# Interleaving a sliding-window attention with its projections from the third head group on instead of the second

## The chip, the core and the metric

The kernel runs on one core of one Trainium2 chip. The metric is the device time of one execution in microseconds (us), as the median of several runs. TensorE (PE, with PEld for its weight loads) multiplies, VectorE (DVE), ScalarE (ACT) and GpSimd (POOL) do the rest, and SyncE (SP) issues the DMAs.

## What is computed

Four decoder layers on 256 tokens of width 1024. Each layer is a half SwiGLU, a token mixer, a second half SwiGLU and a gated input. The mixers are, by layer, HGRN2, mLSTM, sliding-window attention and HGRN2 again. The change lies in layer 2 only, in the attention:

```python
def swa_mixer(x, w_qkv, q_gain, k_gain, sinks, w_o):
    q, k, v = jnp.split(x @ w_qkv, [nq, nq + nk], axis=-1)   # 16 query heads, 4 key heads, 64 wide
    q = rmsnorm(q.reshape(B, T, SW_HEADS, SW_HD), q_gain)
    k = rmsnorm(k.reshape(B, T, SW_KV_HEADS, SW_HD), k_gain)
    ...
    s = jnp.einsum('bnqkgd,bnskd->bnkgqs', qb, kk).astype(jnp.float32) * (SW_HD ** -0.5)
    s = s - slopes[:, :, None, None] * dist
    s = jnp.where(valid[None, :, None, None], s, -jnp.inf)
    probs = jax.nn.softmax(jnp.concatenate([s, sink], axis=-1), axis=-1)[..., :-1]
    o = jnp.einsum('bnkgqs,bnskd->bnqkgd', probs.astype(vv.dtype), vv).reshape(B, T, nq)
    return o @ w_o
```

## The kernel before

**Weights.** All weights stream from memory through four 1 MB buffers (`wraw`), each holding two units. ACT rounds a unit to its high part (`wh`, line 253) and DVE subtracts to get the low part (`wl`, line 254); six units of each fit. The program stays three units ahead of the products. Every projection is then three products: high by high, high by low, low by high.

**The attention stage, function `swa`.** The projections run in this order on PE: keys and values (`gemm_rows(x, 512)`), then the queries of four groups of four heads (`gemm_rows(x, 256)`, 48 products each, lines 275 to 277), then the small input projection (`ple_proj`, 48 products, lines 266 to 268), then the output projection (`out_proj`, 192 products, lines 266 to 268). Groups are counted from 0 here: g = 0 is the first. The output projection needs group g's result at its step k0 = 2g, and forces whatever is missing there (`settle`).

After the products of group g, its results are copied (line 1198), squared (1041), summed by DVE (1044), raised to -1/2 on POOL (line 395, in `rsqrt_mean`), and scaled (1048, 1201, 1204). The attention itself is one generator, `attend`. For each group it transposes the queries (`queries`, PE line 1099, evacuated by ACT line 1101), and for each of two token tiles t takes the softmax: four score products, one per head (PE line 1119), each evacuated by DVE (line 1121), then maximum (1127 to 1131), exponentials on ACT (1134), and division on DVE (1137 to 1141). Up to four softmaxes later, `values` transposes the probabilities (PE 1150, ACT 1152), multiplies by the values (PE 1158) and splits the result for the output projection (ACT 253, DVE 254, destinations `slab`).

**What sets the order.** A queue of generators, `bg`, holds such background work. Every product block calls `tick`, which adds to a credit; `advance` runs the next step of the first generator and takes from the credit what the step yields (a bare `yield` costs 1 / `SW_RATE`, that is 0.4; a block of 48 products of a query group gives 2.0). A yielded number, such as `K_WAIT`, lets that much product work pass before the next step. On top of this the tile framework's scheduler settles the order of the instructions of each engine and puts in the waits. Each engine runs its own list strictly in order.

PSUM for the attention's products are two 512-wide tiles (`mis`). The score products of one softmax share such a tile: four heads of 128 keys in tile t = 0, two of 256 keys per tile for t = 1. The product of the next head in a tile waits until DVE has evacuated the head before it.

Of the kernel before, what the change touches and what calls it, by code (L numbers as in the profile page):

```python
# [41 lines left out]
ML_CAP = 15.0  # L42
SW_H, SW_G, SW_D = 16, 4, 64
AHEAD = 3
K_WAIT, Q_WAIT = 2, 0

N_GAIN = 4

# [72 lines left out]
class Kern:  # L121
# [930 lines left out]
    def swa(self, l):  # L1052
# [43 lines left out]
        def queries(g, qn):  # L1096
            ps = self.misc()
            for i in range(4):
                nc.tensor.transpose(ps[:, i * P:(i + 1) * P], qn[:, i * P:(i + 1) * P], self.ident)
            c = (g % 2) * 512  # L1100
            nc.scalar.activation(qT[g // 2][:, c:c + 512], ps, AF.Copy, scale=self.qg)
            yield
# [64 lines left out]
        def attend():  # L1167

            todo = deque()
            for g in range(SW_H // SW_G):  # L1170
                while g not in qns:
                    yield 0.25
                if Q_WAIT:
                    yield Q_WAIT
                yield from queries(g, qns[g][0])
                for t in range(NT):
                    todo.append((g, t, softmax(g, t)))
                    yield
                    if len(todo) > AHEAD:
                        yield from finish(*todo.popleft())  # L1180
            while todo:
                yield from finish(*todo.popleft())

        def finish(g, t, s):
            yield from values(g, t, s)
            if t == NT - 1:
                done.add(g)
            yield
# [4 lines left out]
        for g in range(SW_H // SW_G):  # L1193
            banks = self.gemm_rows(x, 256)
            self.settle(norm)
            qn = self.s512("qn")
            for t in range(NT):
                nc.scalar.copy(out=qn[:, t * 256:(t + 1) * 256], in_=banks[t][0])
            a = self.head_scales([banks[t][0] for t in range(NT)], rc)
            sa = self.small([P, NT * SW_G], "sa", 3)  # L1200
            nc.vector.reciprocal(out=sa, in_=a)
            s3 = sa.rearrange("p (t h) -> p t h", t=NT)
            sl = self.slopes[:, 4 * g:4 * g + 4].rearrange("p (o h) -> p o h", o=1).broadcast_to([P, NT, SW_G])
            nc.vector.tensor_tensor(out=s3, in0=s3, in1=sl, op=ALU.mult)
            qns[g] = qn, a, sa
            if g == 0:
                self.later(attend())
            outs.append((lambda g=g: g in done, self.tiles(oh[g // 2], ol[g // 2])[2 * (g % 2):][:2]))
        self.ple_proj(l)
# [88 lines left out]
```

## Time and profile before

| | us |
|---|---|
| median of 3 runs | 2115.43 |
| lowest, highest | 2112.28, 2116.8 |
| the profiled execution's own time | 2115.12 |
| its span, first to last instruction | 2113.4 |
| PE busy in the span | 2092.2 (99%) |
| DVE, ACT busy | 1541.4 (73%), 1203.2 (57%) |
| attention stage, from the first query product (1260.87) to the first product after the output projection (1357.37) | 96.5 |
| PE busy in that stage, mean granted clock | 93.94, 0.95 |

Times in the rows are us from the span's start. The profile gives each instruction's start and length; PE products overlap in its pipeline, so that a product is listed with about 0.28 us although the next one starts 0.12 us later. A number in square brackets is the time that the engine stood idle before the row, and what released it. The granted clock is 1.00 at 2.4 GHz and 0.50 at 1.2 GHz.

### The profile page before, as it was taken

To read this page: it belongs to the slowest core of one execution; us is meant where nothing else is said; L and a number is where in the kernel's file an instruction comes from. 1 tells how busy PE (TensorE), PEld (TensorE's weight loads), DVE (VectorE), ACT (ScalarE), POOL (GpSimd) and SP (SyncE) were. 2 spreads that over 40 slices of the span, in tenths; PEclk is the share of its full clock that TensorE was granted. 3 is DMA by queue.
4 is the path that set the end of the run, shared out by engine and by line. 5 is a ranking of instruction groups with operands and counts; after the bars stand their busy time and mean duration, and the time that the engine had idled before them with its cause. 6 is when DMAs were issued, how large, how long until landed. Compare 5 with 4: busy or idle time off the path is not lost.

```text
span 2113.4 us, 30586 instructions
## 1 busy us (share of the span) xinstructions
PE 2092.2 (99%) x12269; PEld 1822.3 (86%) x12269; DVE 1541.4 (73%) x2065; ACT 1203.2 (57%) x1678; POOL 50.7 (2%) x84
## 2 busy tenths in 40 slices
PE   8999999999999999999999999999999999999998
PEld 7888889888888888888888887888888888898887
DVE  8766987776877666776687666777687767967766
ACT  7554655554655556655565546665566545565554
POOL 1000000000000000000000001000000000000000
PEclk9999999999999999999999999999999999999999
DMA  7554345555555544555545552355545554445552
GB/s 285 199 186 179 131 149 181 183 196 184 180 197 182 198 142 164 186 192 190 189 179 183 193 181 91 118 193 182 197 170 193 196 183 156 140 160 182 197 182 78
DMA packets 54000, 372.27 MB, mean 176 GB/s; under 512 B 6368, under 2 KB 7136, under 8 KB 9568
## 3 DMA queue, kind: packets, MB, share of 16 engines
q1 hardware_dynamic: 53712, 370.24, 49.1%
q8 instruction: 96, 1.57, 0.3%
q14 instruction: 48, 0.39, 0.1%
q10 hardware_dynamic: 144, 0.07, 0.0%
HBM read 369.23 MB, written 1.05 MB: 175 GB/s over the span
## 4 chain that ended last, share of the span: by engine, by line
PE 89%; DVE 5%; ACT 2%; issue 2%; POOL 1%; DMA 0%; SPq 0%; DVEq 0%; POOLq 0%; ACTq 0%
PE acc L285 50%; PE acc L286 25%; PE acc L267 2%; PE acc L268 2%; PE acc L266 2%; PE acc L275 2%; PE acc L276 2%; PE acc L277 2%; DVE wl L254 1%; PE mis L735 1%; DVE slab L742 1%; PE mis L1119 1%; DVE slab L748 1%; ACT wh L253 0%; PE mis L431 0%
## 5 line engine op out<-in xcount | busy, mean ns | idle before, releaser
L285 PE MATMUL acc<-x,wh 128*128 128x512 f32 x3384 | 1185.2, 395 | 5.9 <-ACT wh L253 5.8
L254 DVE TENSOR_TENSOR wl<-wraw,wh 128x1024 fp32r<-128x1024 f32 (+1 forms) x693 | 845.2, 1222 | 460.5 <-ACT wh L253 460.2
L253 ACT CAST wh<-wraw 128x1024 fp32r<-128x1024 f32 (+1 forms) x693 | 725.8, 1049 | 757.2 <-PE acc L285 412.7
L286 PE MATMUL acc<-x,wl 128*128 128x256 f32 x3384 | 946.1, 280 | 0.6 <-DVE wl L254 0.5
L285 PEld LDWEIGHTS acc<-x,wh 128*128 128x128 f32 x3384 | 635.4, 188 | 153.2 <-ACT wh L253 5.7
L286 PEld LDWEIGHTS acc<-x,wl 128*128 128x128 f32 x3384 | 638.4, 189 | 2.1 <-DVE wl L254 1.9
L285 PE MATMUL acc<-slab,wh 128*128 128x512 f32 x1152 | 403.9, 394 | 0.0
L286 PE MATMUL acc<-slab,wl 128*128 128x256 f32 x1152 | 321.1, 279 | 0.0
L285 PEld LDWEIGHTS acc<-slab,wh 128*128 128x128 f32 x1152 | 216.0, 187 | 50.4
L286 PEld LDWEIGHTS acc<-slab,wl 128*128 128x128 f32 x1152 | 217.0, 188 | 0.0
L315 DVE TENSOR_TENSOR gu<-acc,gu 128x512 f32<-128x512 f32 x176 | 120.3, 684 | 2.0 <-ACT gu L314 1.4
L314 ACT COPY gu<-acc 128x512 f32<-128x512 f32 x176 | 101.9, 579 | 15.9 <-PE acc L286 15.8
L275 PE MATMUL acc<-wh,x 128*128 128x512 f32 (+1 forms) x272 | 103.9, 382 | 0.0
L277 PE MATMUL acc<-wh,x 128*128 128x512 f32 (+1 forms) x272 | 101.4, 373 | 0.0
L276 PE MATMUL acc<-wl,x 128*128 128x512 f32 (+1 forms) x272 | 101.0, 371 | 0.0
L285 PE MATMUL acc<-wide,wh 128*128 128x512 f32 x256 | 91.8, 394 | 0.0
L266 PE MATMUL acc<-slab,wh 128*128 128x256 f32 x256 | 73.6, 289 | 0.0
L267 PE MATMUL acc<-slab,wh 128*128 128x256 f32 x256 | 73.2, 286 | 0.0
L268 PE MATMUL acc<-slab,wl 128*128 128x256 f32 x256 | 72.8, 285 | 0.0
L286 PE MATMUL acc<-wide,wl 128*128 128x256 f32 x256 | 71.4, 279 | 0.0
L257 ACT ACTIVATE x<-h,gains 128x256 fp32r<-128x256 f32 x128 | 57.5, 502 | 22.2 <-DVE h L490 18.6
L452 DVE TENSOR_TENSOR gu<-gu,rb 128x512 f32<-128x512 f32 x88 | 60.7, 692 | 9.2 <-ACT rb L433 6.7
(246 smaller groups left out, 1795.1 us busy)
## 6 DMA issues: line engine op xcount, KB each, us to landing
wraw<-in_w_all SPq DMA_DIRECT2D x346, 1024.0 KB, 4.8
wraw<-in_w_all SPq DMA_DIRECT2D x7, 512.0 KB, 7.8
pt<-in_pT SPq DMA_DIRECT2D x4, 256.0 KB, 4.2
h<-in_xT SPq DMA_DIRECT2D x3, 256.0 KB, 6.2
outT<-h SPq DMA_DIRECT2D x3, 256.0 KB, 2.4
wraw<-in_w_all SPq DMA_DIRECT2D x2, 256.0 KB, 4.4
h<-in_xT SPq DMA_DIRECT2D x2, 128.0 KB, 3.3
outT<-h SPq DMA_DIRECT2D x1, 128.0 KB, 1.7
```

What stands on the lines that cost most here:

```text
L253: self.nc.scalar.copy(out=hi, in_=src)
L254: self.nc.vector.tensor_tensor(out=lo, in0=src, in1=hi.bitcast(F32), op=ALU.subtract)
L266: mm(ps, wh[:, cs], xh, start=first and opens, stop=False, skip_group_check=True)
L267: mm(ps, wh[:, cs], xl, start=False, stop=False, skip_group_check=True)
L268: mm(ps, wl[:, cs], xh, start=False, stop=last, skip_group_check=True)
L275: mm(ps, xh[:, ts], wh[:, cs], start=first, stop=False, skip_group_check=True)
L276: mm(ps, xh[:, ts], wl[:, cs], start=False, stop=False, skip_group_check=True)
L277: mm(ps, xl[:, ts], wh[:, cs], start=False, stop=last, skip_group_check=True)
L285: mm(ps, wh[:, cs], x, start=first, stop=False, skip_group_check=True)
L286: mm(ps[:, T:], wl[:, cs], x[:, :T], start=False, stop=last, skip_group_check=True)
L314: nc.scalar.copy(out=o3, in_=p4[:, :, 1, :])
L315: nc.vector.tensor_tensor(out=o3, in0=p4[:, :, 0, :], in1=o3, op=ALU.add)
```

## The change

The background generator `attend` is queued behind the products and scaling of query group g = 1, where it was queued behind those of g = 0. It no longer asks for a wait of `Q_WAIT` (which was 0) ahead of every group; instead it yields 0.6 once, behind the transposes of group 0.

```diff
-K_WAIT, Q_WAIT = 2, 0
+K_WAIT, Q_FIRST = 2, 0.6
...
             for g in range(SW_H // SW_G):
                 while g not in qns:
                     yield 0.25
-                if Q_WAIT:
-                    yield Q_WAIT
                 yield from queries(g, qns[g][0])
+                if g == 0:
+                    yield Q_FIRST
                 for t in range(NT):
                     todo.append((g, t, softmax(g, t)))
                     yield
...
-            if g == 0:
+            if g == 1:
                 self.later(attend())
```

No instruction is added or removed; on PE, DVE, ACT and POOL they stand in another order, while SP issues the same DMAs in the same order. The first scores on PE, before: `acc_11443` are the products of group 1, `mis_11484` the transposed queries of group 0, `mis_11503` and `mis_11542` the first scores of tiles t = 0 and t = 1.

```order
L1099 MATMUL mis_11484<-ident,qn_11428 128x128 x4
...
L1119 MATMUL mis_11503<-wide_11260,slab_11261 128x128
...
L1119 MATMUL mis_11542<-wide_11260,slab_11261 128x256
L1119 MATMUL mis_11503<-wide_11260,slab_11261 128x128
```

Here 13 products of group 1 stand between the transposes and the first score, and five between the first score and the next. The same place in the changed kernel, where `acc_11529` are the products of group 2 (group 1's 48 are all through by then):

```order
L1099 MATMUL mis_11540<-ident,qn_11428 128x128 [waits Activation_49]
L1099 MATMUL mis_11540<-ident,qn_11428 128x128 x3
...
L1119 MATMUL mis_11577<-wide_11260,slab_11261 128x128 [waits Activation_49]
...
L1119 MATMUL mis_11577<-wide_11260,slab_11261 128x128 [waits DVE_49]
...
L1119 MATMUL mis_11610<-wide_11260,slab_11261 128x256 [waits PE_49]
```

Now 24 products of group 1 and six of group 2 stand ahead of the transposes, 24 more between the transposes and the first score, five between the first and the second score, one between the second and the third; the second score is of the same tile as the first and waits for DVE.

DVE ahead of the first evacuation, before (group 0's scaling, two weight units, then the evacuations):

```order
L1044 TENSOR_REDUCE oss_11434<-sq_11431 128x8 [waits Activation_49]
L394 TENSOR_SCALAR hs_11436<-oss_11434 128x8 [waits DVE_49]
L1048 TENSOR_TENSOR hs_11436<-hs_11436,rc_11256 128x8 [waits Pool_49]
L1201 RECIPROCAL sa_11440<-hs_11436 128x8 [waits DVE_49]
L1204 TENSOR_TENSOR sa_11440<-sa_11440,slopes 128x8 [waits DVE_49]
L254 TENSOR_TENSOR wl_11592<-wraw_11490,wh_11591 128x1024 [waits PE_49,Activation_49]
L254 TENSOR_TENSOR wl_11683<-wraw_11680,wh_11682 128x1024 [waits DMAHW3_49,Activation_49]
L1121 SCALAR_TENSOR_TENSOR slab_11502<-nd,sa_11440,mis_11503 128x128 [waits DVE_49,PE_49]
```

And in the changed kernel, from the second of those two weight units on:

```order
L254 TENSOR_TENSOR wl_11567<-wraw_11564,wh_11566 128x1024 [waits DMAHW3_49,Activation_49]
L1044 TENSOR_REDUCE oss_11520<-sq_11517 128x8 [waits Activation_49]
L394 TENSOR_SCALAR hs_11522<-oss_11520 128x8 [waits DVE_49]
L1048 TENSOR_TENSOR hs_11522<-hs_11522,rc_11256 128x8 [waits Pool_49]
L1201 RECIPROCAL sa_11526<-hs_11522 128x8 [waits DVE_49]
L1204 TENSOR_TENSOR sa_11526<-sa_11526,slopes 128x8 [waits DVE_49]
L254 TENSOR_TENSOR wl_11672<-wraw_11564,wh_11671 128x1024 [waits PE_49,Activation_49]
L1121 SCALAR_TENSOR_TENSOR slab_11576<-nd,sa_11440,mis_11577 128x128 [waits PE_49]
L254 TENSOR_TENSOR wl_11757<-wraw_11754,wh_11756 128x1024 [waits DMAHW4_49,Activation_49]
L1121 SCALAR_TENSOR_TENSOR slab_11576<-nd,sa_11440,mis_11577 128x128 [waits PE_49]
```

The whole scaling chain of group 1 (`hs_11522`, with its wait for POOL) and one more weight unit now stand ahead of the first evacuation, and another weight unit behind it.

ACT where the output projection begins, in the changed kernel (`pT` are transposed probabilities, `pw` results of the input projection, `slab_11263` the high part of group 0's attention output, which the first output product reads):

```order
L1152 COPY pT_11892<-mis_11887 128x512
L532 COPY pw_11969<-acc_11824 128x512 x2
L253 CAST wh_12016<-wraw_12014 128x1024
L253 CAST slab_11263<-mis_11924 128x2x128
L253 CAST wh_12092<-wraw_12014 128x1024
```

Before, the same cast of `slab_11263` (from `mis_11825`) stood between the two last copies to `pw` (`pw_12021`), ahead of the next weight unit. Now two copies and a weight unit stand between `pT_11892` and it.

From the start of the output projection's step k0 = 6 on, and up to the keys' transposes, the lists of the engines are as they were.

## Rows read from the trace of the kernel before

**Rows 1.** The page: busy time by engine, and the chain by engine.

```profile
PE 2092.2 (99%) x12269; PEld 1822.3 (86%) x12269; DVE 1541.4 (73%) x2065; ACT 1203.2 (57%) x1678; POOL 50.7 (2%) x84
...
PE 89%; DVE 5%; ACT 2%; issue 2%; POOL 1%; DMA 0%; SPq 0%; DVEq 0%; POOLq 0%; ACTq 0%
```

**Rows 2.** Stretches: length, busy per engine (instructions), granted clock, DMA share, GB/s.

```profile
1260.87:1357.37 96.50, 93.94 (x618) 75.17 (x616) 63.15 (x176) 62.87 (x149) 10.99 (x5) 0.95 0.27 97
...
1276.00:1278.00 2.00, 1.96 (x8) 1.54 (x10) 0.72 (x2) 0.00 (x0) 0.00 (x0) 0.58 0.83 340
1286.00:1288.00 2.00, 2.00 (x14) 1.82 (x13) 2.00 (x11) 0.00 (x0) 0.00 (x0) 0.86 0.00 0
1272.30:1276.30 4.00, 2.87 (x17) 2.01 (x16) 3.39 (x7) 1.50 (x2) 0.51 (x1) 1.00 0.19 31
1276.30:1286.60 10.30, 10.30 (x37) 7.13 (x36) 5.58 (x22) 3.01 (x6) 1.64 (x1) 0.50 0.22 91
1328.00:1332.00 4.00, 3.25 (x15) 1.56 (x13) 3.54 (x11) 1.35 (x6) 0.00 (x0) 1.00 0.16 33
1792.00:1796.00 4.00, 2.91 (x21) 2.50 (x20) 3.82 (x7) 1.53 (x2) 0.00 (x0) 1.00 0.40 168
```

**Rows 3.** Timeline of PE from the transposes of group 0 to the second score.

```profile
1270.85 0.61 PE L1099 MATMUL mis<-ident,qn 128*128 128x128 f32 x4
1271.22 0.37 PE L275 MATMUL acc<-wh,x 128*128 128x256 f32 x1
1271.42 0.28 PE L276 MATMUL acc<-wl,x 128*128 128x256 f32 x1
...
1272.73 0.28 PE L275 MATMUL acc<-wh,x 128*128 128x256 f32 x1
1273.85 0.48 PE L1119 MATMUL mis<-wide,slab 64*128 64x128 f32 x2 [0.85 <-ACT slab L1101]
...
1276.04 0.57 PE L1119 MATMUL mis<-wide,slab 64*128 64x128 f32 x2 [0.28 <-DVE slab L1121]
...
1279.21 0.41 PE L277 MATMUL acc<-wh,x 128*128 128x256 f32 x1
```

**Rows 4.** Timeline of ACT behind the products of group 1.

```profile
1279.72 0.65 ACT L1198 COPY qn<-acc 128x256 f32<-128x256 f32 x2 [5.92 <-PE acc L277]
1280.25 0.86 ACT L1041 ACTIVATE sq<-acc,rc 128x256 f32<-128x256 f32 x2
```

**Rows 5.** Timeline of DVE from the sums of group 0 to the first evacuations.

```profile
1270.20 0.69 DVE L1044 TENSOR_REDUCE oss<-sq 128x8 f32<-128x512 f32 x1 [2.34 <-ACT sq L1041]
...
1272.85 0.17 DVE L1048 TENSOR_TENSOR hs<-hs,rc 128x8 f32<-128x8 f32 x1 [1.75 <-POOL hs L395]
...
1273.37 2.35 DVE L254 TENSOR_TENSOR wl<-wraw,wh 128x1024 fp32r<-128x1024 f32 x2
1275.64 0.73 DVE L1121 SCALAR_TENSOR_TENSOR slab<-nd,sa,mis 128x128 f32<-128x128 f32 x2
```

**Rows 6.** Timeline of POOL: the powers of the keys and of group 0.

```profile
1262.97 2.69 POOL L395 TENSOR_TENSOR hs<-hs,mhalf 128x8 f32<-128x8 f32 x1 [5.22 <-DVE hs L394]
1271.17 1.64 POOL L395 TENSOR_TENSOR hs<-hs,mhalf 128x8 f32<-128x8 f32 x1 [5.50 <-DVE hs L394]
```

**Rows 7.** Timelines of PE, ACT and DVE about the start of the output projection.

```profile
1308.35 0.48 PE L1119 MATMUL mis<-wide,slab 64*128 64x128 f32 x2 [0.35 <-DVE slab L1121]
...
1330.51 0.70 PE L1119 MATMUL mis<-wide,slab 64*128 64x256 f32 x2 [0.66 <-DVE slab L254]
...
1313.77 0.37 ACT L253 CAST slab<-mis 128x256 fp32r<-128x256 f32 x1 [0.40 <-PE mis L1158]
1314.04 0.59 ACT L532 COPY pw<-acc 128x512 f32<-128x512 f32 x1
1314.52 1.06 ACT L253 CAST wh<-wraw 128x1024 fp32r<-128x1024 f32 x1
...
1314.87 0.42 DVE L254 TENSOR_TENSOR slab<-mis,slab 128x256 fp32r<-128x256 f32 x1
```

## The prediction

> **What bounds the kernel now.** I read the page first. PE is busy for 99% of the span and makes up 89% of the chain that ended last [rows 1]. So a change of order can only give or cost what PE loses between its products, by waiting or by a slower clock. The 96.50 us of the attention stage hold two such losses [rows 2]. PE is idle for 96.50 - 93.94 = 2.56 us, and the mean granted clock is 0.95 where the rest of the program has 1.00.
>
> The clock is the larger loss. It is full up to 1276.3, 1.2 GHz up to about 1286.6, then full again [rows 2]. The first edge row (2 us at 0.58) holds (1 - 0.58) / 0.5 x 2 = 1.68 us of slow clock, the last one 0.56 us, and 8 us lie between: 10.24 us in all. Half of that, 5.12 us, is lost. Before the fall, in the 4 us from 1272.3, PE was busy for 2.87 us and its weight loads for 2.01 us. PE waited 0.85 us at the first score product and 0.28 us at the second [rows 3]. Neither idleness nor sparse weight loads decide alone, though: the stretches from 1792 (2.91 us busy) and from 1328 (weight loads 1.56 us) kept the full clock [rows 2].
>
> The first wait comes from ACT, which evacuates the transposed queries behind two weight units. The second comes from DVE: its two weight units run from 1273.37 for 2.35 us, so the first evacuation starts only at 1275.64 and the next score may not be written before that [rows 3, 5]. Two later waits of some size, 0.35 and 0.66 us, are of the same kind: a score behind DVE's work on weights [rows 7].
>
> **The change, part by part.** I walk the changed order with the old durations. Up to the transposes at 1270.85 the lists agree.
>
> *Products of group 1 alone.* All 24 that are left now follow each other. One starts every 0.12 us (1271.42 to 1272.73 is 11 of them [rows 3]). The last starts at 1270.85 + 23 x 0.12 = 1273.61 and ends 0.28 later, at 1273.9. Their weights are no concern: they are split three units ahead, and the DMA share is low here (0.19 [rows 2]). The DMA queue keeps its order, so no load is moved past another.
>
> *The first wait goes.* Six products of group 2, from 1273.73, put the transposes at 1274.45. With 0.37 to the next product, 0.20 to the one after it and 0.12 for each further one, 24 products follow to about 1277.7; a change of shape costs some 0.1 more [rows 3]. The first score starts at 1277.9. ACT starts its copies of group 1's result 0.10 after the last product (1279.62 to 1279.72 before), the squares 0.53 later, and needs 1.39 from the first copy to the last square [rows 4]: 1274.0 to 1275.4. The evacuation of the transposes stands right behind; even with 1 us it is done by 1276.4. So there is a slack of 1.5 us where PE waited 0.85. That wait is removed.
>
> *The second wait grows.* DVE is busy with its pair of weight units until 1273.37 + 2.35 = 1275.72, as before. Then come group 1's sums, the wait for POOL, the three scalings and one weight unit, and only then the first evacuation. From the start of the sums to the start of the weight unit group 0 needed 1273.37 - 1270.20 = 3.17 us [rows 5]. So the weight unit runs from 1278.9 to 1280.1 (half of 2.35 us), and the evacuation, half of 0.73 us, ends at 1280.4. On PE the first score ends at 1278.3, and five products bring it to 1279.0. There the second score waits until 1280.4: **1.4 us** in place of 0.28. Behind it stand all of PE's products; nothing can pass. The bounds are 0.28, the wait that the same pair had, and 2.45, if POOL takes the 2.69 us that it took for the keys instead of 1.64 for group 0 [rows 6]. I take 1.4, since DVE has nothing to do beside POOL in the new order, as it had nothing beside the 1.64.
>
> The Trainium skill has a rule for these two durations ("SBUF — State Buffer", section "Who interferes with whom"): a DVE instruction with two inputs in SBUF contends with a GpSimd instruction that reads SBUF. Here a weight split stood right behind the keys' power and none behind group 0's, so the trace agrees; by the rule the wait is 1.4 us, without it 2.45 would be as likely.
>
> *After that* DVE's second weight unit ends at about 1281.5. The third score is one product behind the second, so DVE is there in time, and I find no wait in the next eight scores. Until the output projection the same products and scores must pass on PE, and three more changes of shape (20 for 17) are made up by two fewer behind it (16 for 18). The 0.35 and 0.66 us waits I keep: weight units still stand between evacuations.
>
> *Start of the output projection.* ACT casts group 0's result after two copies to `pw` and a weight unit: 2 x 0.59 + 1.06 + 0.37 = 2.6 us behind the last transposed probabilities [rows 7]. PE has the last value products and a 256-wide score in between, some 1.3 to 1.9 us by the 0.70 us of such a score [rows 7]. The wait is 0.7 to 1.3 us, or nothing if the copies start sooner. ACT was early there before (it idled 0.40 us for PE [rows 7]), so I take 0.7. At the other end the last value products now have ten products (1.2 us) ahead of step k0 = 6; cast and subtraction need 0.37 + 0.42 = 0.8 us [rows 7]. That costs nothing.
>
> *The clock.* The new order moves PE's sparsest piece instead of filling it. From 1277.9 on PE has two scores of 64 rows, five products and 1.4 us of idleness in 3.4 us; before the fall it had 0.85 and 0.28 us of idleness among much the same scores [rows 3]. I take it that the clock falls again, a few us later, and for as long: 5.12 us lost before and after.
>
> **Sum.** The profiled execution took 2115.12 us (span 2113.4). Less 0.85 and 0.28, plus 1.4 and 0.7: 2115.12 + 0.97 = **2116.1 us**. That execution is 0.3 us below the median of 2115.43, which I leave. The difference is +0.03%, no change that can be measured (about 0.2%, 4.2 us, is what a measurement of this kernel can tell). With the bounds of both waits (0.28 to 2.45, 0 to 1.3) this case reaches from 2114 to 2118, with the scatter of the runs from 2112.5 to 2119.
>
> **The rivals.**
>
> *The clock does not fall.* For it: the stretch at 1792, with 2.91 of 4 us busy, kept it [rows 2], and 24 products in a row come just ahead of the sparse piece. Against it: the wait is longer than either of the old ones, and scores that fill only 64 rows of the array (64*128 in [rows 3]) surround it. It gives 2116.1 - 5.12 = 2111.0 us, just faster by the bound of 2111.2.
>
> *The slow clock lasts longer (slower).* The clock rose before while scores were still mixed with products, after a stretch of 10.3 us with 37 recorded products [rows 2]. In the new order the scores of groups 0 and 1 follow each other with few products between: from the second score until group 1's scores are through there are 50 products (6.0 us), 15 scores (0.4 to 0.6 us each, some 7.7), two sets of transposes (0.8) and 14 changes of shape (2.8), 17 us at full clock or 34 at half. So there is room for a longer fall. Twice as long, 20.5 us, it costs another 5.12: 2121.2 us. It decides from about 7.1 us of further slow clock on (3.56 us lost), which takes 2116.1 past the upper bound of 2119.7.
>
> *The new wait is not there.* The copies and squares end early enough for POOL, or the score comes later, and the 1.4 us shrink to 0.28; ACT's cast is in time too. With the same fall: 2115.12 - 0.85 = 2114.3 us. DVE's strict order speaks against it.
>
> That the change does not do what it says is excluded by the order of the instructions.
>
> **How the numbers follow.** The forecast has 0.52, no fall 0.25, the longer fall 0.15, no new wait 0.08. Of "no fall" four fifths lie below 2111.2, and 0.03 of the forecast's case: faster 0.23. The longer fall and 0.03 of the forecast's: slower 0.18. Same: 0.59. The range for 8 in 10 must reach into both clock cases: 2110.0 to 2120.0. The forecast's own is 2112.5 to 2119.
>
> **What would show it.** Right: the first score does not wait for ACT; the second waits 1 to 2 us for DVE near 1279 to 1280.4, with POOL's power for group 1 at about 1.64 us; the mean clock of the stage stays near 0.95, with one fall between 1280 and 1284. Wrong: a stage clock of 1.00 (then 2111), or below 0.92 (then 2120); a first evacuation by DVE ahead of the weight unit; waits of over 2 us in the output projection.

## Result: slower by 0.7%, mostly through TensorE's clock

The changed kernel takes 2129.44 us, median of 7 runs (2125.2 to 2137.09), against 2115.43 us before: a ratio of 1.007, with a 95% interval of 1.0053 to 1.0087. In a second comparison (e11, below) it is 1.0088 (1.0058 to 1.0118). The prediction, 2116.1 us and no measurable change, was wrong, and so was its range, 2110.0 to 2120.0.

The profiled execution took 2128.07 us (span 2126.2), 12.95 us more than the one before. PE still sets the time: its share of the span and its 89% of the chain are those of [rows 1].

```profile
PE 2101.8 (99%) x12269; PEld 1830.4 (86%) x12269; DVE 1541.5 (72%) x2065; ACT 1202.4 (57%) x1678; POOL 49.8 (2%) x84
...
PE 89%; DVE 5%; issue 2%; ACT 2%; POOL 1%; DMA 0%; SPq 0%; DVEq 0%; ACTq 0%; POOLq 0%
```

The stretches of the changed kernel, to be read against [rows 2]: length, busy time of each engine (instructions), granted clock, DMA share, GB/s. The first is the attention stage, between the same two products as before.

```profile
1264.60:1370.30 105.70, 99.83 (x618) 80.19 (x616) 63.13 (x176) 62.80 (x149) 10.11 (x5) 0.89 0.25 89
1280.00:1284.00 4.00, 2.85 (x21) 2.40 (x20) 2.15 (x8) 1.68 (x2) 1.64 (x1) 1.00 0.58 244
1284.00:1288.00 4.00, 3.94 (x15) 2.78 (x16) 2.23 (x5) 0.00 (x0) 0.00 (x0) 0.79 0.78 262
1288.00:1300.00 12.00, 12.00 (x39) 8.83 (x38) 4.95 (x14) 5.09 (x14) 0.00 (x0) 0.50 0.00 0
1316.00:1320.00 4.00, 2.31 (x12) 1.16 (x11) 2.10 (x11) 2.72 (x6) 1.02 (x1) 1.00 0.72 264
1320.00:1328.00 8.00, 8.00 (x31) 5.30 (x31) 5.19 (x12) 5.06 (x14) 0.00 (x0) 0.57 0.00 0
1352.00:1356.00 4.00, 3.29 (x17) 1.78 (x18) 3.08 (x9) 2.58 (x5) 0.00 (x0) 0.83 0.19 27
1356.00:1360.00 4.00, 4.00 (x28) 4.00 (x28) 0.27 (x1) 0.56 (x1) 0.00 (x0) 0.75 0.59 240
```

The stage grew from 96.5 to 105.7 us, by 9.2. PE is idle in it for 105.70 - 99.83 = 5.87 us in place of 2.56: 3.3 us more. The clock falls three times instead of once. The slow clock lasts (1 - 0.79) / 0.5 x 4 + 12 = 13.7 us in the first fall, 6.9 in the second, 1.4 + 2.0 = 3.4 in the third: 24 us against 10.24. Taken as half lost, that is 12.0 against 5.12: 6.9 us more. Both together are 10.2, one more than the stage grew. Half is a little too much: products that start every 0.12 us at full clock start every 0.21 us in the first fall (L275 at 1298.70, L276 at 1298.91), so 44% is lost rather than 50%, and the two together come to 9.3. The remaining 3.7 us stand ahead of the stage (its first product comes at 1264.61 instead of 1260.87), in code that the change does not touch; the last section has them.

The timeline of PE shows what stands ahead of each fall, to be read against [rows 3, 7].

```profile
1281.59 0.48 PE L1119 MATMUL mis<-wide,slab 64*128 64x128 f32 x2
...
1284.06 0.49 PE L1119 MATMUL mis<-wide,slab 64*128 64x128 f32 x2 [1.21 <-DVE slab L1121]
...
1317.61 0.48 PE L1119 MATMUL mis<-wide,slab 64*128 64x128 f32 x2 [0.86 <-DVE slab L1121]
...
1319.25 0.65 PE L1158 MATMUL mis<-pT,s 128*64 128x256 f32 x2 [0.67 <-ACT pT L1152]
...
1341.18 0.39 PE L267 MATMUL acc<-slab,wh 128*128 128x256 f32 x1 [0.85 <-DVE slab L254]
...
1352.46 0.65 PE L1158 MATMUL mis<-pT,s 128*64 128x256 f32 x4 [1.19 <-ACT pT L1152]
```

The first score no longer waits. The second, at 1284.06, waits 1.21 us for DVE, and the clock falls some 2 us later. The other two falls follow the waits at 1317.61 and 1319.25, and the one at 1352.46. The wait at 1341.18 is followed by none. Rows of POOL, DVE and ACT tell where three of the waits come from:

```profile
1280.34 1.64 POOL L395 TENSOR_TENSOR hs<-hs,mhalf 128x8 f32<-128x8 f32 x1 [3.79 <-DVE hs L394]
...
1283.67 0.34 DVE L1121 SCALAR_TENSOR_TENSOR slab<-nd,sa,mis 128x128 f32<-128x128 f32 x1
...
1314.55 2.48 POOL L395 TENSOR_TENSOR hs<-hs,mhalf 128x8 f32<-128x8 f32 x1 [7.00 <-DVE hs L394]
...
1314.31 1.22 DVE L254 TENSOR_TENSOR wl<-wraw,wh 128x1024 fp32r<-128x1024 f32 x1
...
1317.06 0.17 DVE L1048 TENSOR_TENSOR hs<-hs,rc 128x8 f32<-128x8 f32 x1 [1.53 <-POOL hs L395]
...
1317.21 0.34 DVE L1121 SCALAR_TENSOR_TENSOR slab<-nd,sa,mis 128x128 f32<-128x128 f32 x1
...
1351.84 0.57 ACT L1152 COPY pT<-mis 128x512 f32<-128x512 f32 x1
```

At 1284 the first evacuation stood behind group 1's scaling, which waits for POOL, and a weight unit (1282.53 to 1283.75). At 1317 the score's evacuation stood behind a scaling that waited 1.53 us for POOL. At 1352 the copy of the transposed probabilities stood behind four exponentials (1349.40 to 1351.74).

### The profile page after: what moved, and what is told of

It is laid out like the page before. It is cut to its first block, busy times and chain, and to the rows that moved or that the text cites. A ratio compares the mean times of both kernels' runs of the same rounds, so it can differ in the third digit from the quotient of the medians.

```text
span 2126.2 us, 30579 instructions
## 1 busy us (share of the span) xinstructions
PE 2101.8 (99%) x12269; PEld 1830.4 (86%) x12269; DVE 1541.5 (72%) x2065; ACT 1202.4 (57%) x1678; POOL 49.8 (2%) x84
## 4 chain that ended last, share of the span: by engine, by line
PE 89%; DVE 5%; issue 2%; ACT 2%; POOL 1%; DMA 0%; SPq 0%; DVEq 0%; ACTq 0%; POOLq 0%
PE acc L285 49%; PE acc L286 25%; PE acc L267 2%; PE acc L266 2%; PE acc L277 2%; PE acc L275 2%; PE acc L268 2%; PE acc L276 2%; DVE wl L254 1%; PE mis L735 1%; DVE slab L742 1%; PE mis L1119 1%; DVE slab L748 1%; POOL hs L395 0%; PE mis L431 0%
## 5 line engine op out<-in xcount | busy, mean ns | idle before, releaser
L285 PE MATMUL acc<-x,wh 128*128 128x512 f32 x3384 | 1188.3, 396 | 5.8 <-ACT wh L253 5.7
L285 PEld LDWEIGHTS acc<-x,wh 128*128 128x128 f32 x3384 | 635.4, 188 | 154.0 <-ACT wh L253 5.7
L285 PE MATMUL acc<-slab,wh 128*128 128x512 f32 x1152 | 404.8, 394 | 0.0
L285 PEld LDWEIGHTS acc<-slab,wh 128*128 128x128 f32 x1152 | 216.0, 187 | 50.5
L275 PE MATMUL acc<-wh,x 128*128 128x512 f32 (+1 forms) x272 | 104.1, 383 | 0.0
L276 PE MATMUL acc<-wl,x 128*128 128x512 f32 (+1 forms) x272 | 101.4, 373 | 0.0
L285 PE MATMUL acc<-wide,wh 128*128 128x512 f32 x256 | 92.0, 395 | 0.0
```

Of the source, the lines that this page charges most:

```text
L275: mm(ps, xh[:, ts], wh[:, cs], start=first, stop=False, skip_group_check=True)
L276: mm(ps, xh[:, ts], wl[:, cs], start=False, stop=False, skip_group_check=True)
L285: mm(ps, wh[:, cs], x, start=first, stop=False, skip_group_check=True)
```

## The experiments

Four theories were told apart. A: the later start makes PE wait for the other engines, above all in the output projection, and each wait makes the clock fall, whatever the products around it. B: the pause `Q_FIRST` did it, not the later start. C: the score products, which use 64 of the array's 128 rows, hold the clock down. D, formed on the way: a wait begins a fall, and 64-row products draw it out. Every run's record has its span and mean granted clock. Half the clock loses about half the time, so span x (1 - clock) is taken as what slow clock cost a run (by the 44% above, some tenth too much). The record gives the clock in steps of 0.001, that is 2.1 us of a run, so means that differ by 1 us or less are not told apart. The program's last few us run at a slow clock too, but cost little by this count: 0.4 us in the profile of the kernel before (5.40 us at 0.92). In the table, the stage is that of the profiled execution, cut as above; the last column is the mean over the runs, behind the slash that of the kernel before in the same comparison. Its medians there are 2112.37 us (e1 to e4), 2112.72 (e5 to e8) and 2111.11 (e9 to e11). The 2115.43 is from the first comparison.

| kernel | median us | ratio to before (95%) | stage, us | PE idle in it, us | clock in it | lost by the clock, us |
|---|---|---|---|---|---|---|
| before | 2115.43 | 1 | 96.50 | 2.56 | 0.95 | |
| changed | 2129.44 | 1.007 (1.0053 to 1.0087) | 105.70 | 5.87 | 0.89 | 16.4 |
| changed, again (e11) | 2130.53 | 1.0088 (1.0058 to 1.0118) | 109.98 | 5.74 | 0.84 | 17.4 / 4.0 |
| e1 start only | 2116.76 | 1.0012 (0.9995 to 1.0028) | 96.88 | 4.27 | 0.96 | 3.2 / 3.0 |
| e2 pause only | 2115.99 | 1.0017 (1.0002 to 1.0032) | 95.61 | 2.83 | 0.96 | 4.2 / 3.0 |
| e3 changed, 128 rows | 2114.10 | 1.0007 (0.9991 to 1.0023) | 94.67 | 8.25 | 0.96 | 4.1 / 3.0 |
| e4 changed, rate 3.3 | 2121.22 | 1.0039 (1.0023 to 1.0056) | 113.13 | 3.52 | 0.79 | 10.1 / 3.0 |
| e5 before, 128 rows | 2105.93 | 0.9963 (0.9946 to 0.998) | 86.30 | 3.80 | 1.00 | 0.4 / 3.5 |
| e6 changed, deferred | 2125.32 | 1.0056 (1.0038 to 1.0073) | 108.66 | 3.85 | 0.86 | 11.7 / 3.5 |
| e8 pause, 128 rows, deferred | 2108.46 | 0.998 (0.9965 to 0.9994) | 89.08 | 5.84 | 1.00 | 1.9 / 3.5 |
| e10 pause, 128 rows | 2107.44 | 0.9975 (0.9959 to 0.9991) | 88.08 | 5.31 | 1.00 | 0.5 / 4.0 |

### e11: the whole change once more

No edit.

> The changed kernel once more, word for word, beside runs of the kernel before whose clocks are recorded too, so that the difference can be split into the clock's part (the span times one less the granted clock, averaged over the runs) and the rest. From the runs of the first comparison: 2126 to 2131 us, a mean loss by the clock of 14 to 18 us against 3 to 4 us of the kernel before, and 3 us more of everything else.

The mean spans are 2129.7 and 2111.6 us, 18.1 apart. The clock's part is 17.4 - 4.0 = 13.4 us of that, the rest 4.7. So two thirds to three quarters of the slowdown are slow clock (the lower figure with the 44%), about as expected. The first profile (mean clock 0.994, the other six runs of that comparison 0.992) had shorter falls than most; here the stage has its clock at 0.84, behind the same wait of 1.21 us at the second score.

```profile
1259.44:1369.42 109.98, 104.24 (x617) 83.21 (x615) 63.37 (x176) 62.76 (x149) 10.10 (x5) 0.84 0.23 86
```

### e1 and e2: one half of the change each

```diff
 e1, in the changed kernel
-                if g == 0:
-                    yield Q_FIRST
 e2, in the changed kernel
-            if g == 1:
+            if g == 0:
                 self.later(attend())
```

> One half of the change alone: the attention's steps start at the second group's queries (g == 1), but the pause Q_FIRST behind the first group's transposes is left out, so seven products stand between these transposes and the first score, in place of over twenty. Theory A (the later start squeezes the attention into the output projection, TensorE waits there for VectorE's and ScalarE's copies, and each idle spell is followed by a fall of the clock): the waits of 0.86 us and 1.19 us in the output projection stay, with about three falls and over 18 us of slow clock in the stage; 2125 to 2131 us. Theory B (the pause is what made it slower, by moving the evacuations of the first scores in among the weights' work on VectorE): near the kernel before, one fall, 2113 to 2119 us. Theory C (the 64-row score products hold the clock down wherever they stand, the waits matter little): slow clock of about 24 us as in the changed kernel, and no link between the falls and the waits.

> The other half alone: the attention starts at the first group's queries as in the kernel before, with the pause of 0.6 steps between the first group's transposes and its first score. Theory A (the later start): the first score no longer waits for ScalarE, the output projection keeps the kernel before's waits of 0.66 us and less, one fall or none; 2110 to 2118 us. Theory B (the pause): a wait of over 1 us of the second score for VectorE, more than one fall, 2122 to 2130 us. Theory C: slow clock as long as in the kernel before (10 us) or more, whatever the waits.

Neither half does it: both lie within 0.2% of the kernel before, and their loss by the clock is within 1.2 us of its. So A's figure for e1 was a miss, B's for e2, and C's 24 us of slow clock for e1. C's slow clock for e2, as long as before or longer, is not refuted: the mean loss is 4.2 us against 3.0, though its profile has only two falls of 3.4 us. What each avoids shows at the second score. In e1 it does not wait at all: the first evacuation stands ahead of group 1's scaling on DVE. The third score of that tile waits 0.36 us, and the clock stays up through the following scores; a longer wait later is followed by a short fall (PE's timeline, then two stretches):

```profile
1278.62 0.49 PE L1119 MATMUL mis<-wide,slab 64*128 64x128 f32 x2
...
1281.56 0.49 PE L1119 MATMUL mis<-wide,slab 64*128 64x128 f32 x2 [0.36 <-DVE slab L1121]
...
1313.44 1.09 PE L1119 MATMUL mis<-wide,slab 64*128 64x256 f32 x4 [1.65 <-DVE slab L1121]
```

```profile
1281.00:1301.00 20.00, 19.64 (x124) 15.53 (x123) 16.08 (x52) 12.95 (x39) 1.44 (x1) 1.00 0.16 54
1313.00:1325.00 12.00, 11.56 (x56) 8.72 (x56) 8.36 (x19) 6.15 (x15) 0.00 (x0) 0.72 0.49 176
```

In e2 the second score waits 0.51 us:

```profile
1274.08 0.48 PE L1119 MATMUL mis<-wide,slab 64*128 64x128 f32 x2 [0.51 <-DVE slab L1121]
```

Only both halves together put the first evacuation, and with it the second score, behind group 1's sums, POOL's power and a weight unit: 1.21 us.

### e4 and e6: fewer waits, the same rows

```diff
 e4, in the changed kernel
-SW_RATE = 2.5
+SW_RATE = 3.3
 e6, in the changed kernel: rc, reciprocal and slopes move from behind the projection into the attention
                 yield from queries(g, qns[g][0])
                 if g == 0:
                     yield Q_FIRST
+                scales(g)
...
```

> The changed kernel with the attention's steps 3.3 in place of 2.5 for each step of the products beside them: it starts as late but is spread less towards the end. Theory A: the first wait of 1.2 us near the second score and its fall stay, those of the output projection (0.86 us and 1.19 us) and their two falls (10 us of slow clock, 5 us lost) go; 2119 to 2124 us. Theory C: the same slow clock as in the changed kernel, 2126 to 2131 us. Theory B: no change either, since the pause stands as it was: 2126 to 2131 us.

> The changed kernel with its 64-row products, but with the three small VectorE steps that need GpSimd's power (the product with rc, the reciprocal, the product with the slopes) moved from right behind the group's projection to behind its transposes in the attention, so that VectorE splits weights while GpSimd works. The score's waits for VectorE (1.21 us near 1284, 0.86 us near 1317, 0.44 us near 1337) should go or fall below 0.4 us each; those for the copy of the exponentials (0.67, 1.19 us) stay. Theory A: with two of three waits gone, two of three falls go; the clock's loss drops from 16 us to 5 or less and the time to 2114 to 2119 us. Theory C: the products' rows and their order are as before, so the clock's loss stays at 12 to 18 us, and the time drops by the waits alone, 2 us: 2124 to 2129 us.

Both took PE's idleness down, to 3.52 and 3.85 us, well below the changed kernel's 5.87. e4 by itself speaks for A: its median, 2121.22 us, lies where A had it, and its mean loss of 10.1 us is some 6 us below the changed kernel's. C's figure was too high. But its profiled execution, the slowest of the twelve, has the lowest clock of all, with little idleness: two falls of some 30 and 17 us. In e6 A's figure was a miss and C's time, 2124 to 2129 us, a hit: the waits of 0.86 and 1.19 us are gone, one of 1.04 us came in the output projection, with no fall behind it, and the clock still costs 11.7 us. And e1, with more idleness than either, 4.27 us, loses 3.2. So the amount of waiting doesn't decide. In e6 one wait, again at the second score, is followed by 28 us and more at 1.2 GHz without a further wait:

```profile
1281.46 0.48 PE L1123 MATMUL mis<-wide,slab 64*128 64x128 f32 x2 [1.21 <-DVE slab L1125]
```

```profile
1285.00:1313.00 28.00, 28.00 (x91) 20.94 (x92) 14.20 (x46) 10.84 (x28) 1.67 (x1) 0.50 0.01 6
```

I had expected this wait to go too. But here the edit did not change DVE's order: group 1's product with rc still waits for POOL's power ahead of the first evacuation, which is group 0's and doesn't need it. (For group 2 the product did move, to 9.5 us behind the power's start.)

```profile
1279.40 0.17 DVE L1052 TENSOR_TENSOR hs<-hs,rc 128x8 f32<-128x8 f32 x1 [1.75 <-POOL hs L395]
...
1281.06 0.34 DVE L1125 SCALAR_TENSOR_TENSOR slab<-nd,sa,mis 128x128 f32<-128x128 f32 x1
```

So no run takes away this wait alone: that it begins the long fall is read from four profiles in which it stands ahead of one (changed, e11, e4, e6) and from e1 and e2, which have neither this wait nor a fall of over 7 us in their profiles. Its length does not set the fall's: behind 1.19 to 1.21 us the falls last from 13.7 to some 30 us.

### e3 and e5: scores on all 128 rows

The keys lie in two tiles, one with zeros in the lower 64 rows and one in the upper; the two heads' queries stand in one set of weights. The products keep their number, columns and order; copies of the keys on ACT and fills of zeros on POOL come in.

```diff
-        kT = self.wide()
+        kT = [self.wide() for _ in range(2)]
...
-                nc.tensor.matmul(ps[:, c:c + nk], qT[g // 2][r, q0:q0 + P], kT[r, g * T:g * T + nk],
+                nc.tensor.matmul(ps[:, c:c + nk], qT[g // 2][:, q0:q0 + P], kT[hh % 2][:, g * T:g * T + nk],
```

> The changed kernel, with its order kept, but each score product uses all 128 rows of the array: the keys lie in two tiles, one with zeros in the lower 64 rows and one with zeros in the upper 64, and the queries of both heads are the weights. The products' number and columns stay; one more copy per block of keys on ScalarE and two fills of zeros on GpSimd come in. Theory C (64-row products hold the clock down): the falls go or become much shorter, the stage gives back up to 11 us of the 12 us that its slow clock costs, 2115 to 2121 us, while the waits of about 1.2, 0.9 and 1.2 us stay. Theory A (the waits): three falls and some 24 us of slow clock stay, 2126 to 2132 us.

> The kernel before, with its order kept, and score products on all 128 rows as in e3. Theory C (what keeps the clock down are the 64-row score products; a wait at most begins a fall): runs without slow clock become the rule, so that the mean loss by the clock, 3.0 us in the kernel before, goes below 1 us, and the time is 2 to 3 us below the kernel before: 2108 to 2111 us. Theory A (waits alone): the wait of 0.85 us before the first score stands as before, and so does the fall behind it: no difference, 2111 to 2114 us.

This is the edit that brings the clock back. In e3 PE is idle for 8.25 us, more than in any other kernel here, with one wait of 2.23 us; yet it shows about 7 us of slow clock in its profile, and the clock costs 4.1 us instead of 16.4, the mean of the first seven runs of the changed kernel. In e5 it costs 0.4 us, though the wait of 0.86 us at the first score stands as in [rows 3] and a later score waits 1.23 us for DVE, as long as the second score of the changed kernel. The stages of e3 and e5, and these waits:

```profile
1262.18:1356.85 94.67, 86.42 (x617) 74.65 (x615) 63.19 (x176) 63.78 (x151) 10.11 (x5) 0.96 0.28 99
```

```profile
1282.28 0.59 PE L1122 MATMUL mis<-wide,slab 128*128 128x128 f32 x2 [2.23 <-DVE slab L1124]
```

```profile
1259.47:1345.77 86.30, 82.50 (x617) 72.30 (x615) 63.04 (x176) 64.16 (x151) 11.92 (x5) 1.00 0.31 109
```

```profile
1273.24 0.49 PE L1122 MATMUL mis<-wide,slab 128*128 128x128 f32 x2 [0.86 <-ACT slab L1105]
...
1298.68 0.49 PE L1122 MATMUL mis<-wide,slab 128*128 128x128 f32 x2 [1.23 <-DVE slab L1124]
```

The two kernels also show what the changed order costs without 64-row products: e3 is 0.44% slower than e5 by their ratios to the kernel before (1.0007 and 0.9963, in two comparisons), some 9 us, with 4.45 us more idleness and 3.7 us more lost by the clock. So padding takes away about half of what the change costs, not all.

e5 is faster than both kernels, by more than C allowed. Its stage is 10.2 us shorter than before, of which the profiled fall explains only 5.12. e7 points to the rest.

### e7: 64 rows where PE never waits

```diff
 in mm_t, for the first feed-forward layer of layer 3
-        mm(ps, wh[:, cs], x, ...)
+        mm(ps, wh[r, cs], x[r], ...)     r: the upper 64 rows in three stretches, else all
```

> The disputed cost by itself, in a place where TensorE waits for nothing: in the first feed-forward layer of layer 3 (the profile's stretch from about 1575 us on) the kernel before uses only the upper 64 rows of weights and activations (it leaves the lower half of these sums out) in three stretches of 48 pairs of products, about 17 us each: in every pair, in every second, and in every fourth. Nothing else changes; a product of 64 rows has the same columns. Theory C: the clock falls in the first stretch without any wait before it and stays low until 128-row products return, and less or not at all in the two thinner ones; 2118 to 2125 us. Theory A: the clock stays at 1.00 in all three, and the time is the kernel before's.

The kernel leaves out half of the sums in these stretches, so only its time is of use. C in its plain form falls, and both times were missed. The clock stays at 1.00 in all three stretches. These are (every pair, every second, every fourth):

```profile
1578.00:1590.00 12.00, 12.00 (x69) 10.30 (x69) 9.98 (x12) 9.12 (x13) 0.00 (x0) 1.00 0.65 240
1610.00:1634.00 24.00, 24.00 (x89) 13.12 (x90) 12.10 (x14) 8.89 (x12) 0.00 (x0) 1.00 0.36 132
1654.00:1670.00 16.00, 16.00 (x74) 10.78 (x74) 9.62 (x11) 6.41 (x9) 0.00 (x0) 1.00 0.51 188
```

The kernel is slower all the same, 2127.07 us against 2112.72. 64-row products alone run as fast as full ones: 69 in 12 us, 0.35 us a pair. In the second stretch, where 64 and 128 rows alternate from pair to pair, 24 us hold 89 products, 0.54 us a pair. So each change of the number of rows costs 0.19 us here. 48 changes in the second stretch and 24 in the third make 72 x 0.19 = 13.7 of the 14.35 us. The Trainium skill ("TensorEngine Tiling (Array Packing)", section "Key Properties") says that a change of the tiling mode, not of the tile alone, drains the engine. The trace agrees as to the time and gives it a price; the drain itself isn't seen, since PE counts as busy throughout. In e5's stage 10.2 - 5.12 us, plus the 1.24 us of idleness that it has more, are 6.3 us. The trace of the kernel before has 54 changes between 64 and 128 rows in its stage, which makes 0.12 us each: an estimate, lower than e7's price, and that these changes are the whole of the 6.3 us is not shown.

### e8 and e10: candidates

e10 is e2 with e3's scores; e8 adds e6's deferral.

> All that the runs so far favour, in one kernel: the attention starts at the first group's queries as before, with the pause of 0.6 steps before its first score (e2), score products on 128 rows (e3), and the small VectorE steps moved behind the transposes (e6). Waits in the stage below 1.5 us in total and no slow clock: 2106 to 2110 us under theory C, some 3 us or 0.15% below the kernel before. Under theory A the same, since the waits are gone too. If only the waits counted it would equal e5 less 1 us.

> e8 without the moved VectorE steps: the attention starts at the first group's queries, the pause of 0.6 steps stands before the first score, score products have 128 rows. Theory C and D: no slow clock in nearly all runs, and the waits of e2 (2.6 us in the stage, near the kernel before's); 2104 to 2108 us, equal to e5 within 2 us. If it is 2 us or more below e8, the moved VectorE steps are what made e8 slower than e5. Theory A: falls as in e2 (mean loss by the clock 4 us), 2110 to 2114 us.

Both beat the kernel before, and neither beats e5. Both times are as expected, the waits are not: below 1.5 us in total was expected of e8, and 2.6 of e10. The clock's loss is 1.9 and 0.5 us; what they have more than e5 is idleness (5.84 and 5.31 against 3.80 us), mostly scores that wait for DVE (3.4 and 3.5 us against 1.9), and in e8 1.5 us of the clock. e10 is only 1.0 us below e8, less than the intervals can tell, so the deferral is not shown to matter.

### e9, e12 and e13: rows and waits apart

The kernel of e5, whose attention keeps its clock, gets extra f32 products in layer 3's first feed-forward layer, in four stretches of ten blocks.

```diff
 in front of every fourth pair; r is 64 or all 128 rows, by stretch
+            for c in range(2):
...
+                nc.tensor.matmul(ps[:, c * T:(c + 1) * T], y[r, :P], y[r, T:], start=True, stop=True)
...
 e12, e13, after the fifth block of a stretch (w columns); e9 has only the copy and transposes, in two stretches
+                nc.vector.tensor_copy(out=s, in_=ps)
+                nc.vector.tensor_tensor(out=s[:, :w], in0=s[:, :w], in1=s[:, :w], op=ALU.mult)
+                nc.gpsimd.tensor_tensor(out=s[:, :w], in0=s[:, :w], in1=self.mhalf[:, :w], op=ALU.pow)
...
+                nc.tensor.transpose(ps[:, :P], s[:, :P], self.ident)
```

> The parts apart, where nothing else disturbs: e5's kernel, whose attention showed no slow clock, with products added to the first feed-forward layer of layer 3 (from about 1570 us on; their results are read by nobody). Before every fourth pair, two products of 256 columns in full f32, like the scores', in four stretches of ten such blocks: the first stretch with 64 rows, the second with 128 rows, the third with 64 rows and one wait of TensorE for a VectorE copy after the fifth block, the fourth with 128 rows and one such wait. Theory C as it stands after e7 (64-row f32 products between 128-row products lower the clock by themselves): falls in the first and the third stretch, none in the second and fourth. Theory A (a wait alone makes a fall): falls behind the waits of the third and fourth stretch only. Theory D (it takes both: a wait begins the fall, 64-row products let a small wait do it and draw it out): a fall in the third alone. Time: some 45 us of added products over e5, and 2 to 5 us for each fall.

e9 (2147.27 us) had no wait in it: other products had been drawn ahead of the transposes. So it says only that 64-row f32 products among 128-row ones, without waits, keep the clock at 1.00 (from 1575 to 1730 us PE is idle nowhere).

> e9 with waits of TensorE that its order of work can't slip past (in e9 the products behind had been drawn ahead, so that TensorE waited nowhere). The same four stretches of ten blocks of f32 products, one block in front of every fourth pair: the first and the third stretch with 64 rows, the second and the fourth with 128. After the fifth block of each, a transpose waits for a power on GpSimd of that block's result: of 8 columns in the first two stretches (a wait of about 1 us, like the kernel's own), of 16 in the last two (about 2 us). Theory D (it takes a wait and 64-row products together): falls of the clock in the first and the third stretch, none in the second, and in the fourth none or a shorter one. Theory A (a wait alone): falls in all four, or in the third and fourth by the wait's length. If there is no fall in any, a single wait of 1 to 2 us between dense products is not what makes the clock fall in the attention, and it takes what else is there: several short products and gaps close together. Time about 2147 us, plus the waits and 2 us and more for each fall.

> e12 with the rows of the stretches exchanged (the first and the third block stretch with 128 rows, the second and the fourth with 64) and all four waits made by a power of 16 columns, so that each place is seen with either size and waits of about 2.5 to 3.5 us. Theory D: falls in the second and the fourth stretch (64 rows), none in the first and the third, although the third has the longest wait (3.42 us in e12). Theory A: a fall behind the third stretch's wait, as in e12, whatever the rows. Time about 2155 to 2165 us.

e12 took 2161.32 us and e13 2171.42, more than the 2155 to 2165 expected of it. The four waits of e12 (64, 128, 64, 128 rows) and the 16 us behind each:

```profile
1582.76 0.33 PE L494 MATMUL mis<-ident,pT 128*128 128x128 f32 x1 [1.22 <-POOL pT L492]
1615.58 0.33 PE L494 MATMUL mis<-ident,pT 128*128 128x128 f32 x1 [1.50 <-POOL pT L492]
1651.04 0.33 PE L494 MATMUL mis<-ident,pT 128*128 128x128 f32 x1 [3.42 <-POOL pT L492]
1691.28 0.33 PE L494 MATMUL mis<-ident,pT 128*128 128x128 f32 x1 [2.70 <-POOL pT L492]
```

```profile
1583.00:1599.00 16.00, 16.00 (x77) 11.98 (x77) 6.85 (x8) 5.46 (x7) 0.00 (x0) 1.00 0.21 71
1615.00:1631.00 16.00, 15.42 (x84) 13.49 (x85) 7.11 (x8) 4.74 (x6) 0.53 (x1) 1.00 0.24 87
1651.00:1667.00 16.00, 15.96 (x44) 10.83 (x45) 2.47 (x3) 2.58 (x3) 0.00 (x0) 0.57 0.09 37
1691.00:1707.00 16.00, 15.72 (x86) 13.79 (x87) 7.93 (x9) 5.36 (x7) 1.13 (x2) 1.00 0.34 125
```

The same of e13 (128, 64, 128, 64 rows):

```profile
1583.36 0.33 PE L494 MATMUL mis<-ident,pT 128*128 128x128 f32 x1 [2.74 <-POOL pT L492]
1618.31 0.33 PE L494 MATMUL mis<-ident,pT 128*128 128x128 f32 x1 [2.22 <-POOL pT L492]
1658.60 0.33 PE L494 MATMUL mis<-ident,pT 128*128 128x128 f32 x1 [3.64 <-POOL pT L492]
1694.17 0.47 PE L494 MATMUL mis<-ident,pT 128*128 128x128 f32 x1 [2.50 <-POOL pT L492]
```

```profile
1583.00:1599.00 16.00, 15.64 (x77) 13.52 (x78) 6.66 (x8) 5.30 (x7) 0.31 (x1) 0.89 0.19 68
1618.00:1634.00 16.00, 15.70 (x50) 10.84 (x51) 3.33 (x5) 2.48 (x4) 0.25 (x1) 0.68 0.17 65
1658.00:1674.00 16.00, 15.40 (x74) 13.31 (x75) 5.66 (x6) 4.25 (x5) 0.54 (x1) 0.89 0.30 115
1694.00:1710.00 16.00, 15.83 (x59) 11.11 (x60) 4.49 (x5) 3.79 (x5) 1.02 (x2) 0.79 0.19 66
```

With (1 - clock) / 0.5 x 16, the falls among 64-row blocks last 10.2, 6.7 and 13.8 us, behind waits of 2.22, 2.50 and 3.42 us. Among 128-row blocks they last 3.5, 0 and 3.5 us, behind 2.74, 2.70 and 3.64 us. Waits of 1.22 and 1.50 us are followed by no fall with either. So at longer waits the 128-row blocks have the shorter falls, in either order of the places. That is D, with two misses: its first wait in e12, among 64 rows, is followed by no fall, and in e13 the waits start short falls with 128 rows too, where D expected none. A misses the fall behind e12's last wait, and has its fall behind e13's third.

Three things stay open. In the attention with 64-row scores falls follow waits of 1.21 us, among dense feed-forward products none follows one of that size; transposes, value products and several waits lie close together there, and they were not taken apart. And a 64-row block brings two changes of the number of rows with it, so whether the rows or the changes draw the fall out was not separated. And these are two profiles: since falls behind like waits differ much from one execution to the next in the attention, the weight of the 128 rows lies on e3 and e5, with 12 and 11 runs, more than on e12 and e13.

## Why the prediction was wrong

**The first wait goes.** Right: at 1281.59 the first score starts without one.

**The second wait grows.** Right: 1.21 us, against 1.4 from the walk. POOL's power took 1.64 us as taken, DVE's weight unit stood from 1282.53 and the evacuation behind it at 1283.67.

**The later waits are kept.** Too small. In place of the 0.35 and 0.66 us stand 0.86 and 0.44. The 0.86 comes from POOL's power for group 3, which took 2.48 us with a weight unit on DVE beside it, against 1.64 for group 1. New are 0.85 us in the output projection and 1.19 us at its last value products. There the prediction had looked at the cast and subtraction, and called it free; what came last was the copy of the probabilities, behind four exponentials. At the start of the output projection PE waits for nothing, where 0.7 us stood in the sum: PE ran at half clock there, and ACT waited 0.92 us for it. A wait of 0.67 us stands ahead of it. All in all PE idles 3.3 us more, where the sum had 1.0.

**The clock falls again, and for as long.** This is the step that failed. The clock's loss is the largest term, 5.12 us, and was taken over unchanged, with one profile as its evidence. In its place the runs show 13.4 us more (e11; 6.9 in the profiled execution). They show too that the fall is no constant of the kernel. The kernel before lost between nothing and some 10 us from run to run (clocks of 1.000 to 0.995), 3 to 4 us on average; its profiled execution, with 5.5 us, was on the unlucky side. The changed kernel loses 16.4 and 17.4 us on average. The rival with a longer fall named what fits the runs best, sparse scores close together, and got 0.15; it had one fall of 20.5 us, where there were three with 24 us and, in e11, 34 us. Its sum had 0.2 us for a change of shape where the walk had 0.1; e7 has 0.19, and the estimate for the attention 0.12.

**What would show it.** The stage's clock of 0.89 is below the 0.92 named as the mark of the wrong case, for which 2120 us was given.

## What to carry to other kernels

- Here the price of a short wait of TensorE among sparse 64-row products was less the wait than the slow clock behind it. Read the granted clock of every stage, and over several runs: one profile shows one draw.
- Products of 64 rows, strewn among full ones, cost time at each change: 0.19 us in e7. Where the operands allow it, try padding them with zeros to full rows: here that makes the kernel before 0.37% faster (0.9963, 0.9946 to 0.998), more than any order of the steps tried here.
- Two moves that are harmless alone can meet on one engine's queue. Here each alone cost less than 0.2%, and both together 0.7 to 0.9%. Follow the queue with both applied, to the last step of the stage.

## What the runs showed of the hardware beyond that

Of the 3.7 us ahead of the stage, 3.2 arise in one feed-forward layer, from about 575 to 745 us into the program. A pair of their products takes 347 ns in some stretches and 353 in others, at a clock of 1.00, and a kernel's layers don't keep to one of the two. In the stretch from 600 to 720 us the starts give 346.7 ns in the kernel before and 353.3 ns in the changed one (here the products of L285 in each):

```profile
600.00:720.00 120.00, 120.00 (x347) 64.93 (x347) 1.00 0.53 187
```

```profile
600.00:720.00 120.00, 120.00 (x341) 63.79 (x340) 1.00 0.53 188
```

That is 1.9%, some 3 us over the 168 us of one such layer. What chooses between them was not found. It could account for much of the scatter of either kernel, which was not tested, and it is a reason not to explain differences of a few us from single profiles.
